# A hybrid decoder step on one core: shorter inverse roots, a one-instruction softmax bias, the MLP's first product in a written order, and new orders for all engines

## The chip, the cores and the metric

The kernel runs on one core of a Trainium2 chip. The metric is the device time of one execution in microseconds (us), median of several runs. Below, PE is TensorE's matmul queue, ACT is ScalarE, DVE is VectorE, POOL is GpSimd, and SP is the queue from which most DMAs are issued.

## The reference

One layer, for 256 prompt tokens and 8 sequences of 8 sample tokens, width 1024, all in float32:

```
h  = rmsnorm(x);  q, k, v, z, xbc, dt = h @ W_in
attention: MoBA, 8 heads of 64. A query scores the mean key of each past block of 256 tokens, keeps
           the best 3 and its own block, and takes softmax(q k) v over those. The prompt attends to
           itself, a sample sequence to 1024 past tokens (paged cache) and to itself. q, k: rmsnorm, rotary
ssd:       Mamba-2: causal convolution of width 4, silu, chunked scan over 8 heads of 64 (state 128)
           with a state carried in and out; y * silu(z), rmsnorm
x1 = x  + concat(attention, ssd) @ W_out
x2 = x1 + cross_attention(rmsnorm(x1), rmsnorm(mem)) @ W_o     (4 heads of 128, 256 memory tokens)
y  = x2 + relu(rmsnorm(x2) @ W_up)**2 @ W_down                 (width 4096)
```

It returns y for both groups, the new keys and values, the memory's keys and values, and the new convolution and ssd states.

## The kernel before

**Tiling.** Activations lie transposed, 128 features on the partitions by T = 320 tokens, eight tiles for the width of 1024. A weight chunk (`wr`, 128x1024, 512 KB) is loaded by a DMA on SP's or ACT's queue (`load`, L335), rounded to fp32r by ACT (`wh`, L387), and the rest is taken by DVE (`wl`, L388). `gemm3` forms hi*hi, hi*lo and lo*hi, so a product with one output tile is 24 matmuls (L393 to L395) of 128x320, given out as four units of six. Activations are split the same way by `split` (ACT L530, DVE L531). The values come first, in `V` units (L710 to L714). The first kernel rows also do the table load for ACT's exponential (L318) and warm-up matmuls (L538, fed by a POOL memset).

**Norms.** The scale of an rmsnorm isn't applied to the input but to the product: sums of squares are gathered on DVE (`acc`, L491), summed over partitions on PE (`means`, L498), and `rsqrt` takes the inverse root on DVE: an integer guess (L470), then three Newton rounds of three instructions (L472 to L474), on tiles of 3 to 24 columns. `spread` turns the columns into a row over all partitions with PE (L371). `qk_factors` does this for x (units F0 to F2) and for the heads of q (F3 to F5: `to_tokens` copies the sums on ACT at L509 and L511 and transposes them on PE, L371; then `rsqrt`, a copy at L611, and PE's `spread`) and of k (F6 to F9, the same with `dt_part`, L729 and on, between). `cross_factors` (X) does it for the cross attention's heads, `gated_norm` and `memory` have one root each, and `up_factor` the last, of x2.

**Order.** Each part of the work is a generator whose steps are units of PE work. `ORDER` is a string with one letter a unit; `weave_by` takes the next unit of the letter's generator, so PE's order is written out by hand. The letters that matter here: F `qk_factors`, Q the q and k products, V values, S `sample_attn`, T `prompt_attn`, B xbc products and their convolution, D and R the ssd, X `cross_factors`, G the product qx and then ox. Where a unit is numbered below (B28), it is counted from 0 in its generator. DVE's, ACT's and the DMAs' orders are written as runs of numbers (`DVE_ORDER`, `ACT_ORDER`, `DMA_ORDER`), which `_issue_order` makes into dependencies. POOL's order is free. All DMAs take turns on eight semaphores, so one waits for the landing of that eight places earlier, and a DMA on ACT's queue holds up what follows there.

**The MLP.** Up to the residual after ox everything comes from `ORDER`. The up product runs in `weave("", ...)`: a planner gives out the units of `up_factor` (F) and `G_up` (G) by estimated durations and lags. The first four products are held in PSUM (two buffers of `mm`, two of `as`) until the factor `rb3` is there, then `up_done` empties them: DVE relu and scale (`t`), ACT the square rounded (`hh`), POOL the square (L1683), DVE the rest (`hl`). From product 9 on each product also takes one step of `states_sample`, which updates the sample's ssd states. The down product follows.

**The sample attention's bias** is made in `sample_attn` by two DVE instructions, the maximum times -0.125 (L891) and that added to the block bias (L892).

Of the kernel before, what the change touches and what calls it, by code (L numbers as in the profile page):

```python
# [13 lines left out]
ALU = mybir.AluOpType  # L14
# [33 lines left out]
for _n, _c in (("g_mix", 8), ("g_x", 8), ("g_mem", 8), ("g_mlp", 8), ("g_ssm", 4),  # L48
# [40 lines left out]
DVE_ORDER = ("0+2 17 4 3 5 18 6+1 19 8 10+1 9 12+1 20 14+1 21 16 22+2 27 32 35 25+1 36 28 30 29 31 53 33+1 37 39 38 40+8 54 "  # L89
# [161 lines left out]
def _body(tc, nc, I, O):  # L251
# [215 lines left out]
    def rsqrt(out, x):  # L467

        t = ti(out.shape[-1])
        V.tensor_scalar(out.bitcast(I32), x.bitcast(I32), -0.5, MAGIC, op0=ALU.mult, op1=ALU.add)  # L470
        for _ in range(3):
            V.scalar_tensor_tensor(t, out, -0.5, out, op0=ALU.mult, op1=ALU.mult)  # L472
            V.tensor_tensor(t, t, x, op=ALU.mult)
            V.scalar_tensor_tensor(out, t, 1.5, out, op0=ALU.add, op1=ALU.mult)  # L474
# [1289 lines left out]
```

## Time and profile before

| | |
|---|---|
| median of 3 runs | 514.2 us (513.79 to 515.15) |
| the profiled execution's own time | 513.36 us |
| its span in the profile | 511.6 us |
| busy: PE, PE weight load | 499.2, 452.5 us |
| busy: DVE, ACT, POOL | 342.1, 252.4, 47.8 us |
| granted TensorE clock | 0.999 |
| read and written | 109.71 MB and 6.14 MB |

Busy times are sums over the records of each engine; PE's matmuls are pipelined, so a record is longer than the step from one start to the next. The profile lists waits by the releaser that came last, and a timeline row ends with the engine's idle time before it and what ended that. Stretches by window: the values and q, k products to 65 us, both attentions, convolution and ssd to 170, the mixer's output to 215, the memory and the cross attention to 280, and the MLP from there on.

### The profile page before, as it was taken

Reading aid. Unit: us, or ns where it says so; the run is one execution under the profiler, and the core shown is the slowest. Engines: PE = TensorE matmul, PEld = TensorE weight load, DVE = VectorE, ACT = ScalarE, POOL = GpSimd, SP = SyncE. Lnnn points to the kernel's source line nnn. Section 1 sums busy time; section 2 is a strip of 40 time slices with the busy share of each in tenths; the row PEclk is TensorE's granted clock in tenths of the full one; section 3 lists DMA queues with packets and bytes.
Section 4 is the critical chain, followed back from the end, with each engine's and each line's share of the span. In section 5 each row is a group of like instructions: output and inputs, shape, how many; then the busy total and the mean of one; then the engine's idle time right before and its main releaser. Section 6 shows DMA issues by size and latency. Waiting matters only on the chain.

```text
span 511.6 us, 10525 instructions
## 1 busy us (share of the span) xinstructions
PE 499.2 (98%) x3954; PEld 452.5 (88%) x3954; DVE 342.1 (67%) x697; ACT 252.4 (49%) x520; POOL 47.8 (9%) x90
## 2 busy tenths in 40 slices
PE   8999999999999999999999999999999999999997
PEld 5978777877767789999688999999999999999997
DVE  6868799685787799955749778766766433433431
ACT  8534436958667956635566344334344233232330
POOL 2500000030100000000000124222221000000000
PEclk9999999999999999999999999999999999999999
DMA  8999999899899155895904475554644455554530
GB/s 285 318 366 357 368 346 328 306 379 377 285 395 376 66 166 177 285 357 175 400 7 124 124 273 184 179 192 163 207 164 132 157 178 141 173 174 149 170 96 13
DMA packets 45364, 116.53 MB, mean 228 GB/s; under 512 B 5058, under 2 KB 7234, under 8 KB 45314
## 3 DMA queue, kind: packets, MB, share of 16 engines
q1 hardware_dynamic: 39266, 94.37, 54.1%
q10 hardware_dynamic: 6048, 21.50, 11.7%
q8 instruction: 31, 0.51, 0.4%
q14 instruction: 19, 0.16, 0.1%
HBM read 109.71 MB, written 6.14 MB: 226 GB/s over the span
## 4 chain that ended last, share of the span: by engine, by line
PE 84%; ACT 6%; DVE 5%; DMA 2%; issue 1%; SPq 0%; ACTq 0%; DVEq 0%
PE mm L393 22%; PE mm L394 21%; PE mm L395 21%; PE as L925 2%; PE sc L872 2%; DMA wr<-w 2%; PE ms L371 2%; PE as L371 1%; ACT wh L387 1%; DVE wl L388 1%; PE sc L710 1%; PE sc L1546 1%; PE sc L1548 1%; PE as L1570 1%; PE mm L1620 1%
## 5 line engine op out<-in xcount | busy, mean ns | idle before, releaser
L387 ACT ACTIVATE wh<-wr 128x1024 fp32r<-128x1024 f32 (+1 forms) x115 | 118.9, 1037 | 173.6 <-PE mm L394 103.8
L388 DVE TENSOR_TENSOR wl<-wr,wh 128x1024 fp32r<-128x1024 f32 (+1 forms) x115 | 144.1, 1256 | 83.0 <-ACT wh L387 81.0
L393 PE MATMUL mm<-big,wh 128*128 128x320 f32 x544 | 172.2, 316 | 0.8 <-DVE t L991 0.8
L395 PE MATMUL mm<-big,wl 128*128 128x320 f32 x544 | 168.1, 309 | 0.0
L394 PE MATMUL mm<-big,wh 128*128 128x320 f32 x544 | 168.1, 309 | 0.1
L393 PEld LDWEIGHTS mm<-big,wh 128*128 128x128 f32 x544 | 102.2, 188 | 9.7 <-issue 5.9
L394 PEld LDWEIGHTS mm<-big,wh 128*128 128x128 f32 x544 | 102.3, 188 | 0.8 <-DVE big L1608 0.3
L395 PEld LDWEIGHTS mm<-big,wl 128*128 128x128 f32 x544 | 102.1, 188 | 0.1
L395 PE MATMUL mm<-hh,wl 128*128 128x320 f32 x256 | 78.9, 308 | 0.0
L394 PE MATMUL mm<-hl,wh 128*128 128x320 f32 x256 | 78.9, 308 | 0.0
L393 PE MATMUL mm<-hh,wh 128*128 128x320 f32 x256 | 78.9, 308 | 0.0
L394 PEld LDWEIGHTS mm<-hl,wh 128*128 128x128 f32 x256 | 48.0, 188 | 0.0
L393 PEld LDWEIGHTS mm<-hh,wh 128*128 128x128 f32 x256 | 48.0, 188 | 0.0
L395 PEld LDWEIGHTS mm<-hh,wl 128*128 128x128 f32 x256 | 48.0, 188 | 0.0
L1683 POOL TENSOR_TENSOR t<-t 128x320 f32<-128x320 f32 x32 | 28.4, 887 | 160.9 <-DVE t L1680 152.0
L1680 DVE SCALAR_TENSOR_TENSOR t<-mm,rb 128x320 f32<-128x320 f32 x32 | 15.7, 489 | 15.1 <-PE mm L395 14.7
L1684 DVE TENSOR_TENSOR hl<-t,hh 128x320 fp32r<-128x320 f32 x32 | 15.4, 481 | 3.1 <-POOL t L1683 3.1
L872 PE MATMUL sc<-kv,qs 128*32 128x256 f32 x256 | 16.1, 382 | 0.4 <-DVE m L876 0.4
L1681 ACT ACTIVATE hh<-t 128x320 fp32r<-128x320 f32 x32 | 14.7, 458 | 3.7 <-DVE t L1680 3.7
L998 DVE SCALAR_TENSOR_TENSOR t<-t,cwh,t 128x320 f32<-128x320 f32 x24 | 13.2, 549 | 4.4 <-ACT t L996 2.3
L1346 DVE TENSOR_TENSOR x2T<-mm,x2T 128x320 f32<-128x320 f32 x8 | 3.9, 492 | 17.8 <-PE mm L395 17.8
L925 PE MATMUL as<-kv,p 128*32 128x256 f32 x256 | 15.3, 382 | 0.0
(356 smaller groups left out, 619.4 us busy)
## 6 DMA issues: line engine op xcount, KB each, us to landing
wr<-w SPq DMA_DIRECT2D x69, 512.0 KB, 3.5
wr<-w ACTq DMA_DIRECT2D x41, 512.0 KB, 4.8
kv<-ckT SPq DMA_DIRECT2D x64, 256.0 KB, 5.1
kv<-cv SPq DMA_DIRECT2D x64, 256.0 KB, 6.0
kv<-mk SPq DMA_DIRECT2D x8, 512.0 KB, 5.2
kv<-mv SPq DMA_DIRECT2D x8, 512.0 KB, 6.9
kv<-h SPq DMA_DIRECT2D x4, 512.0 KB, 8.0
big<-h SPq DMA_DIRECT2D x4, 512.0 KB, 5.1
```

The costliest lines, as they stand in the source:

```text
L371: PE.transpose(out, in_, ident[:n, :n])
L387: A.activation(hi[:, c], raw[:, c], AF.Copy)
L388: V.tensor_tensor(lo[:, c], raw[:, c], hi[:, c], op=ALU.subtract)
L393: PE.matmul(out, hi[:, cols], xh, start=start, stop=False)
L394: PE.matmul(out, hi[:, cols], xl, start=False, stop=False)
L395: PE.matmul(out, lo[:, cols], xh, start=False, stop=stop)
L872: PE.matmul(ps[r:r + 32, 256 * n:256 * n + 256], qs[:, s, g, b0 + e, :], kbs[e][:, :, 128 * (2 * g + s):128 * (2 * g + s) + 128], start=s ...
L925: PE.matmul(yv[r:r + 32, 0:256], pT[:, 2 * n + q, r:r + 32], vbs[e][:, q, 256 * g:256 * g + 256], start=n == 0 and q == 0, stop=first and ...
L1680: V.scalar_tensor_tensor(t, ps[:, :T], 0.0, rb3, op0=ALU.max, op1=ALU.mult)
L1681: A.activation(hh[:, m, :], t, AF.Square)
L1683: G.tensor_tensor(f, t, t, op=ALU.mult)
L1684: V.tensor_tensor(hl[:, m, :], f, hh[:, m, :], op=ALU.subtract)
```

## The change

1. `rsqrt` takes 8 instructions for 10: a first step with a quadratic correction (four instructions) and a second with a scaled Newton round (three).
2. The softmax bias is one instruction (L901 after), with the maximum broadcast; only the first of the four groups of sequences keeps the separate product.
3. The up product, the up factor and the states' steps are streams of `ORDER`: `!` opens the MLP's buffers, `u` gives the units of products 0, 2 and 4 to 31, `w` those of 1 and 3, `r` the factor, `t` the states. `up_done` is called at once where the factor is there, and otherwise by the second `r` unit.
4. POOL's order is written too (`POOL_ORDER`), and all other orders are new.

Lines after stand 6 to 10 below those before. In the core of the diff the tables of numbers are left out:

```diff
-ORDER = ("FVVVVQQQQQQQQQQQQQVQQFVQFVFQFQQQFVQQQQQSSQQQFSSQQQZQZSSFSFSVSSQFFBBBBSZBSBFBBSBBTZSBSSBBBSSBBTBTTBBS"
-         "SBSBSSBBSSSBTSSTBZSZBBSSBBTBTSZBBTSTBDSSSSZSDZSZDDZDSSZSDSDDSDTDDZZDDSDSZDDSZRSSSSSRSSRRMORORWRORWRO"
...
-         "cbabbaacMbcaddcddadcdGGKGGGGWGGGGGGGGGGG")
+ORDER = ("VFVVVQQQQQQQQQQQQQQVQFVQFQVFQFQQQFVQQQQSSQQQFSSQQQZQZSSFSFSVSSQFFBBBBSZBSZBBSFBBTBBSSSBBBSSBBTBTBBTS"
+         "SBSBBSSBSSSBSTSTBZSZBBSSBTBBZBBTSDBZSSDSSSTSZSZDDZTDSSZSDDSDDSDTDZZDDSDSZDDSZRSSSSSRRSRRSMOOROWRRWOR"
...
+         "babbXaaMbccdadcdddacdGGGGGGKGGGGGWGGGGGG!uuuwuruuuuwwrwwwwuwuuuuuuuuuuuuuuuuuuuutuuuuuuuutuuutuuuuuu"
+         "uuuuuuutuuutuuuuutuuutututuuuuuuutuuuuutuuuuuuuuuutuuuttuuutuuutuuutuuuuuuuuuuuuuuuuuuuu")
...
+POOL_ORDER = ("13 0+1 3 5 8 4 7 11 2 6 12 18 9+1 14 26 15+2 25 19+2 23+1 22 28 27 46 29 32 31 30 35+1 47 34 37 33 44 38+2 42 "
...
         V.tensor_scalar(out.bitcast(I32), x.bitcast(I32), -0.5, MAGIC, op0=ALU.mult, op1=ALU.add)
-        for _ in range(3):
-            V.scalar_tensor_tensor(t, out, -0.5, out, op0=ALU.mult, op1=ALU.mult)
-            V.tensor_tensor(t, t, x, op=ALU.mult)
-            V.scalar_tensor_tensor(out, t, 1.5, out, op0=ALU.add, op1=ALU.mult)
+        V.scalar_tensor_tensor(t, out, -0.5, out, op0=ALU.mult, op1=ALU.mult)
+        V.tensor_tensor(t, t, x, op=ALU.mult)
+        V.scalar_tensor_tensor(t, t, 5.0 / 3, t, op0=ALU.add, op1=ALU.mult)
+        V.scalar_tensor_tensor(out, t, 1.25, out, op0=ALU.add, op1=ALU.mult)
+        V.scalar_tensor_tensor(t, out, -1.6875, out, op0=ALU.mult, op1=ALU.mult)
+        V.tensor_tensor(t, t, x, op=ALU.mult)
+        V.scalar_tensor_tensor(out, t, 2.25, out, op0=ALU.add, op1=ALU.mult)
...
         V.reduce_max(t1, m5[:, 0:n5], axis=AX.X)
-        V.tensor_scalar(t1, t1, -0.125, None, op0=ALU.mult)
-        V.tensor_scalar(b5[:, 0:n5], b5[:, 0:n5], t1, None, op0=ALU.add)
+        V.scalar_tensor_tensor(b5[:, 0:n5], t1.broadcast_to((P, n5)), -0.125, b5[:, 0:n5], op0=ALU.mult, op1=ALU.add)
+        if first:
+            V.tensor_scalar(t1, t1, -0.125, None, op0=ALU.mult)
...
-    def states_sample(first):
-
-
+    def states_sample():
+
+        yield {"mlp"}, 0
...
                 V.tensor_tensor(by_head(h2), by_head(h2), el_s[:, 8 * c:8 * c + 8, None].broadcast_to((P, 8, 64)), op=ALU.mult)
-                yield
+                yield 0, 0
                 V.tensor_tensor(h2, h2, hps[q], op=ALU.add)
                 S.dma_start(O["ssm_s"][c], h2)
-                yield
+                yield 0, 0
 
...
-    weave(ORDER, F=qk_factors(), X=cross_factors(), S=att[0], N=norm(), D=ys[0], R=ys[1], T=att[1], a=crs[0], b=crs[1], c=crs[2], d=crs[3],
-          M=memory(), Q=G_mixer(), V=G_v(), B=G_xbc(), Z=G_z(), O=G_oa(), J=G_os(), G=G_all(), K=G_kx(), W=G_vx())
-    x3h, x3l = x4[0][:, 0], x4[0][:, 1]
-    xT = x2T[0]
-    xe_ = made["xe"]
-    rt3 = tl(xe_, [P, 3], "rt3")
-    rb3 = tl(xe_, [P, T], "rb3")
+    stD = ExitStack()
+    mlp = {}
+    def to_mlp():
+        p1s.close()
+        pm = pool("mlp", st=stD, side="right", reuse_waits="tile")
+        mlp["h"] = tl(pm, [P, 32, T], "hh", F32R), tl(pm, [P, 32, T], "hl", F32R)
+        mlp["rt"] = tl(made["xe"], [P, 3], "rt3")
+        mlp["rb"] = tl(made["xe"], [P, T], "rb3")
+        told.add("mlp")
+        yield 0, 0
     def up_done(m):
         def done(ps):
+            hh, hl = mlp["h"]
             t = tm(T)
-            V.scalar_tensor_tensor(t, ps[:, :T], 0.0, rb3, op0=ALU.max, op1=ALU.mult)
+            V.scalar_tensor_tensor(t, ps[:, :T], 0.0, mlp["rb"], op0=ALU.max, op1=ALU.mult)
             A.activation(hh[:, m, :], t, AF.Square)
             f = tm(T)
             G.tensor_tensor(f, t, t, op=ALU.mult)
             V.tensor_tensor(hl[:, m, :], f, hh[:, m, :], op=ALU.subtract)
         return done
-    p1s.close()
-    stD = ExitStack()
-    pm = pool("mlp", st=stD, side="right", reuse_waits="tile")
-    hh = tl(pm, [P, 32, T], "hh", F32R)
-    hl = tl(pm, [P, 32, T], "hl", F32R)
+    late = []
     def up_factor():
-        yield 0, 1.5
+        yield {"mlp"}, 0
         x = ti(3)
         means(x, rsq, T)
-        rsqrt(rt3, x)
+        rsqrt(mlp["rt"], x)
         yield 0.65, 3.0
-        ps = spread(lambda t: rt3[:, t:t + 1].broadcast_to((P, P)), range(3))
-        A.activation(rb3, ps[:, :T], AF.Copy)
+        ps = spread(lambda t: mlp["rt"][:, t:t + 1].broadcast_to((P, P)), range(3))
+        A.activation(mlp["rb"], ps[:, :T], AF.Copy)
         told.add("rb3")
+        for m, ps in late:
+            up_done(m)(ps)
         yield 0.45, 0
-    def G_up():
-        late = []
-        for m in range(32):
-            done = up_done(m)
-            if "rb3" not in told:
-                yield from gemm(CH["up"] + m, tiles(x3h), tiles(x3l), T, late.append, al=mm if m < 2 else sa_ps)
-                if "rb3" in told or m == 3:
-                    yield {"rb3"}, 0
-                    for i, ps in enumerate(late):
-                        up_done(i)(ps)
-                continue
-            yield from gemm(CH["up"] + m, tiles(x3h), tiles(x3l), T, done)
-            if m >= 9:
-                next(states, None)
-    states = states_sample(3)
-    weave("", F=up_factor(), G=G_up())
+    def G_up(ms_):
+        yield {"mlp"}, 0
+        for m in ms_:
+            def done(ps, m=m):
+                if "rb3" in told:
+                    up_done(m)(ps)
+                else:
+                    late.append((m, ps))
+            yield from gemm(CH["up"] + m, tiles(x4[0][:, 0]), tiles(x4[0][:, 1]), T, done, al=mm if m < 2 or m > 3 else sa_ps)
+    weave(ORDER, F=qk_factors(), X=cross_factors(), S=att[0], N=norm(), D=ys[0], R=ys[1], T=att[1], a=crs[0], b=crs[1], c=crs[2], d=crs[3],
+          M=memory(), Q=G_mixer(), V=G_v(), B=G_xbc(), Z=G_z(), O=G_oa(), J=G_os(), G=G_all(), K=G_kx(), W=G_vx(),
+          **{"!": to_mlp(), "r": up_factor(), "u": G_up([0, 2] + list(range(4, 32))), "w": G_up([1, 3]), "t": states_sample()})
+    xT = x2T[0]
+    hh, hl = mlp["h"]
...
+                       (lambda i: i.engine == mybir.EngineType.Pool, POOL_ORDER),
```

Three places. On ACT, the start of the program: `tab` is the tile on which the table is loaded early, `prm` the norms' weights, `big` the split input, L478 (L487 after) a sum of squares. Before:

```order
L340 DMA prm_81<-prm 128x8
L318 ACT_TABLE_LOAD
L318 ACTIVATE tab_78<-tab_78 128x1
L530 ACTIVATE big_116<-big_84,prm_81 128x320
L478 ACTIVATE acc_188<-big_84 128x320
L387 ACTIVATE wh_118<-wr_87 128x512
L530 ACTIVATE big_116<-big_84,prm_81 128x320
L478 ACTIVATE t_191<-big_84 128x320
L552 ACTIVATE kv_117<-big_116 128x2x64
```

After:

```order
L346 DMA prm_81<-prm 128x8
L539 ACT_TABLE_LOAD
L539 ACTIVATE big_116<-big_84,prm_81 128x320
L393 ACTIVATE wh_118<-wr_87 128x512
L539 ACTIVATE big_116<-big_84,prm_81 128x320
L487 ACTIVATE t_199<-big_84 128x320
L393 ACTIVATE wh_118<-wr_87 128x512
L561 ACTIVATE kv_117<-big_116 128x2x64
L487 ACTIVATE acc_196<-big_84 128x320
```

The first ACTIVATE was that on `tab`, which needs nothing but a memset; now it is the first split, which reads `prm`, and the table load comes with it. Sums of squares stand behind the second weight half.

On ACT around F3 and F4, `s` (L509, L511; L518, L520 after) being the copy of q's sums that the transposes of F4 read, and L335 (L341) a weight DMA. Before:

```order
L387 ACTIVATE wh_544<-wr_542 128x1024
L639 ACTIVATE rb_179<-ms_428 128x320
L478 ACTIVATE sq_420<-mm_348 128x320
L335 DMA wr_743<-w 128x1024
L509 ACTIVATE s_82_452<-ms_447 128x320
L511 ACTIVATE s_82_452<-ms_447 128x64
L335 DMA wr_768<-w 128x1024
L387 ACTIVATE wh_583<-wr_581 128x1024
```

After:

```order
L393 ACTIVATE wh_446<-wr_444 128x1024
L648 ACTIVATE rb_179<-ms_426 128x320
L341 DMA wr_739<-w 128x1024
L393 ACTIVATE wh_512<-wr_510 128x1024
L487 ACTIVATE sq_418<-mm_348 128x320
L518 ACTIVATE s_86_463<-ms_458 128x320
L520 ACTIVATE s_86_463<-ms_458 128x64
L341 DMA wr_764<-w 128x1024
L393 ACTIVATE wh_579<-wr_577 128x1024
```

The DMA just ahead of the copies has moved ahead of a weight copy and a square.

On DVE around T0, `tq` with `cst` (L780; L789 after) being the mask added to the prompt attention's scores, which empties their PSUM, L991 (L1001) and L998 (L1008) a convolution's evacuation and its taps. Before:

```order
L991 TENSOR_TENSOR t_1063<-mm_1029,rb_179 128x40x8
L388 TENSOR_TENSOR wl_1289<-wr_1286,wh_1288 128x1024
L956 SCALAR_TENSOR_TENSOR yn_937<-yn_937,ab_1011,ts_1082 128x256
L998 SCALAR_TENSOR_TENSOR t_1068<-t_1063,cwh_158,t_1068 128x320 x3
L780 TENSOR_TENSOR tq_1127<-ms_1104,cst_82 128x384
L780 TENSOR_TENSOR tq_1130<-ms_1105,cst_82 128x384
L780 TENSOR_TENSOR tq_1135<-as_1106,cst_82 128x384
L780 TENSOR_TENSOR tq_1138<-as_1107,cst_82 128x384
L1010 SCALAR_TENSOR_TENSOR t_1168<-mm_767,rb_179 128x320
```

After:

```order
L394 TENSOR_TENSOR wl_1283<-wr_1280,wh_1282 128x1024
L966 SCALAR_TENSOR_TENSOR yn_931<-yn_931,ab_1005,ts_1068 128x256
L1011 SCALAR_TENSOR_TENSOR big_84<-t_991,t_985 128x320
L1001 TENSOR_TENSOR t_1077<-mm_1023,rb_179 128x40x8
L394 TENSOR_TENSOR wl_1391<-wr_1388,wh_1390 128x1024
L789 TENSOR_TENSOR tq_1127<-ms_1104,cst_82 128x384
L789 TENSOR_TENSOR tq_1130<-ms_1105,cst_82 128x384
L789 TENSOR_TENSOR tq_1135<-as_1106,cst_82 128x384
L789 TENSOR_TENSOR tq_1138<-as_1107,cst_82 128x384
L790 TENSOR_REDUCE pmx_202_1124<-tq_1130 128x3
```

A second weight split has come in just ahead of the masks, and the convolution's taps and z's evacuation have moved away from there.

More of the change, by code (lines that the diff above doesn't have):

```diff
@@ L69 @@
 PACE = 1.3
-ORDER = ("FVVVVQQQQQQQQQQQQQVQQFVQFVFQFQQQFVQQQQQSSQQQFSSQQQZQZSSFSFSVSSQFFBBBBSZBSBFBBSBBTZSBSSBBBSSBBTBTTBBS"
-         "SBSBSSBBSSSBTSSTBZSZBBSSBBTBTSZBBTSTBDSSSSZSDZSZDDZDSSZSDSDDSDTDDZZDDSDSZDDSZRSSSSSRSSRRMORORWRORWRO"
-         "OWNOOWNONOOOOOMOONNOWONJJJJJJJJZJJJJJMWJJKOJKKKKKKKKKKGKKKKKWGMXGacJMGGGGGGGMGWGGGGGGMXXbcXXaabcadcb"
-         "cbabbaacMbcaddcddadcdGGKGGGGWGGGGGGGGGGG")
-ACT_ORDER = ("1 0 2 19 3+1 20 6 5 7 21 8+1 22 10+5 23 18 16+1 24+2 28 30 33 32 27 37 34 29 47 38 31 50 41 48 36 35 57 39+1 "
[14 rows of a table removed]
-DVE_ORDER = ("0+2 17 4 3 5 18 6+1 19 8 10+1 9 12+1 20 14+1 21 16 22+2 27 32 35 25+1 36 28 30 29 31 53 33+1 37 39 38 40+8 54 "
[18 rows of a table removed]
-DMA_ORDER = ("0+15 19+1 16+2 21+2 29+1 27 31+6 28 38+16 64 24 55+1 65 25 66 57+4 75 26 62 67+6 84 74 76+7 63 86+1 85 88+3 "
[4 rows of a table removed]
+ORDER = ("VFVVVQQQQQQQQQQQQQQVQFVQFQVFQFQQQFVQQQQSSQQQFSSQQQZQZSSFSFSVSSQFFBBBBSZBSZBBSFBBTBBSSSBBBSSBBTBTBBTS"
+         "SBSBBSSBSSSBSTSTBZSZBBSSBTBBZBBTSDBZSSDSSSTSZSZDDZTDSSZSDDSDDSDTDZZDDSDSZDDSZRSSSSSRRSRRSMOOROWRRWOR"
+         "OWNOOWNONOOOOOMOONNOOWNJJJJJJJJJJMJZJJWJJKJKKKKKKKKKKKKKKKWGGOGGMaXcGJMGGGGGMGWGGGGGGMXXbcXaabcadcbc"
+         "babbXaaMbccdadcdddacdGGGGGGKGGGGGWGGGGGG!uuuwuruuuuwwrwwwwuwuuuuuuuuuuuuuuuuuuuutuuuuuuuutuuutuuuuuu"
+         "uuuuuuutuuutuuuuutuuutututuuuuuuutuuuuutuuuuuuuuuutuuuttuuutuuutuuutuuuuuuuuuuuuuuuuuuuu")
+ACT_ORDER = ("1+3 20 5+1 19 21 7 0 8+2 22 11+3 16+1 23 15 24 28 30 33 18 27 25 32 26 29 38 34 43 37 31 50 39 36 57 44 35 "
[15 rows of a table added]
+DVE_ORDER = ("0+3 17 4+1 18 6+1 9 8 19 10 12 14+1 13 11 20+1 27 32 25 22 26 35 23 28 16 30 36 31 29 51 24 33 37 34 39+1 38 "
[19 rows of a table added]
+DMA_ORDER = ("1+2 0 4+11 19+1 16+2 21+1 29+4 23 34+1 24 36 28 37+5 45 43 46 44 47+6 64 54 25+1 55+3 65 59+2 27 66 62 75 67+4 "
[5 rows of a table added]
+POOL_ORDER = ("13 0+1 3 5 8 4 7 11 2 6 12 18 9+1 14 26 15+2 25 19+2 23+1 22 28 27 46 29 32 31 30 35+1 47 34 37 33 44 38+2 42 "
+              "45 43 49 41 48 50+1 53 52 54+31")
 TAKEN = []
@@ L1226, in states_sample @@
                 S.dma_start(hb[:, b:b + 2, :], I["h0"][b:b + 2].rearrange("b p c -> p b c"))
-        for _ in range(first):
-            yield
+        yield 0, 0
         for e in range(2):
@@ L1241, in states_sample @@
                 V.tensor_tensor(by_head(h2), by_head(h2), el_s[:, 8 * c:8 * c + 8, None].broadcast_to((P, 8, 64)), op=ALU.mult)
-                yield
+                yield 0, 0
                 V.tensor_tensor(h2, h2, hps[q], op=ALU.add)
                 S.dma_start(O["ssm_s"][c], h2)
-                yield
+                yield 0, 0
     def gated_norm():
@@ L1666, in _body @@
     ys = all_of("y", ssd_all(), ssd_rest())
-    weave(ORDER, F=qk_factors(), X=cross_factors(), S=att[0], N=norm(), D=ys[0], R=ys[1], T=att[1], a=crs[0], b=crs[1], c=crs[2], d=crs[3],
-          M=memory(), Q=G_mixer(), V=G_v(), B=G_xbc(), Z=G_z(), O=G_oa(), J=G_os(), G=G_all(), K=G_kx(), W=G_vx())
-    x3h, x3l = x4[0][:, 0], x4[0][:, 1]
-    xT = x2T[0]
-    xe_ = made["xe"]
-    rt3 = tl(xe_, [P, 3], "rt3")
-    rb3 = tl(xe_, [P, T], "rb3")
+    stD = ExitStack()
[7 more added lines that the diff above has]
+        told.add("mlp")
+        yield 0, 0
     def up_done(m):
         def done(ps):
+            hh, hl = mlp["h"]
             t = tm(T)
-            V.scalar_tensor_tensor(t, ps[:, :T], 0.0, rb3, op0=ALU.max, op1=ALU.mult)
+            V.scalar_tensor_tensor(t, ps[:, :T], 0.0, mlp["rb"], op0=ALU.max, op1=ALU.mult)
             A.activation(hh[:, m, :], t, AF.Square)
```

75 rows, old and new, of tables (ACT_ORDER, DMA_ORDER, DVE_ORDER) are left out of this document.

## The prediction

> **What bounds the kernel now.** I read the page's head first, for who is busy, then the stretches of the span, then the list of waits of TensorE, and then the timeline at each place where TensorE waits.
>
> ```profile
> span 511.6 us, 10525 instructions
> PE 499.2 (98%) x3954; PEld 452.5 (88%) x3954; DVE 342.1 (67%) x697; ACT 252.4 (49%) x520; POOL 47.8 (9%) x90
> ...
> PE 84%; ACT 6%; DVE 5%; DMA 2%; issue 1%; SPq 0%; ACTq 0%; DVEq 0%
> ```
>
> The first line is the span, the second each engine's busy time, the third the chain of work that ended last. TensorE is idle for 511.6 - 499.2 = 12.4 us, and that is all a new order can win, since the diff adds and removes no matmul. By stretch (TensorE's busy time stands after the length; the DMA share stands second from the right):
>
> ```profile
> 36.00:70.00 34.00, 31.35 (x296) 24.98 (x297) 27.16 (x88) 14.00 (x32) 1.08 (x5) 1.00 1.00 365
> ...
> 285.00:512.00 227.00, 223.21 (x1538) 221.84 (x1536) 122.86 (x149) 76.25 (x93) 28.40 (x32) 1.00 0.50 159
> ```
>
> From 285 us on, the MLP, TensorE misses 227.00 - 223.21 = 3.8 us, nearly all of it after its last matmul, where the diff touches nothing. The places to look at lie before. These are TensorE's waits by releaser (in total, times, longest; left out are the warm-up's own and one of 0.2 us that no term uses):
>
> ```profile
> PE ms L371 <- ACT s L509: 1.8, 2, 1.2
> PE ms L371 <- DVE ts L611: 1.4, 2, 0.8
> ...
> PE ms L498 <- DVE acc L491: 1.0, 1, 1.0
> PE mm L393 <- DVE t L991: 0.8, 1, 0.8
> PE as L371 <- DVE tq L780: 0.5, 1, 0.5
> PE sc L872 <- DVE m L876: 0.4, 1, 0.4
> PE as L713 <- ACT big L530: 0.4, 1, 0.4
> PE ms L1077 <- ACT rx L1056: 0.3, 1, 0.3
> ...
> PE as L371 <- ACT yn L960: 0.2, 1, 0.2
> PE ms L1077 <- ACT gm L1196: 0.2, 1, 0.2
> ```
>
> No row of TensorE names a DMA. A dozen single waits hold about 8 us, each for ScalarE or VectorE, engines busy for half and two thirds of the span. So the time is set by whether a small result is early enough, and order decides it. A wait costs about 0.16 more than its row, because a matmul's record outlasts its turn (0.31 against the 0.15 from one start to the next); I add 0.16 where I price one, and a unit of a product, six such matmuls, takes 0.88.
>
> ```profile
> 140.16 0.31 PE L393 MATMUL mm<-big,wh 128*128 128x320 f32 x1
> 140.31 0.31 PE L394 MATMUL mm<-big,wh 128*128 128x320 f32 x1
> ```
>
> **The change, part by part.** All sums are against the profiled execution, 513.36 us (span 511.6 and 1.76 around it). The median of the runs shown is 514.2, 0.8 above it.
>
> *Factors F3 to F5.* PE's L371 at 38.28 spreads a factor that ScalarE (L509) copies late, because that copy stands behind a weight DMA on ScalarE's own queue:
>
> ```profile
> 37.41 0.33 ACTq L335 DMA_DIRECT2D wr<-w  x1
> ...
> 37.79 0.44 ACT L509 ACTIVATE s<-ms 128x320 f32<-128x320 f32 x1 [3.05 <-DMA wr<-w]
> ...
> 38.28 0.55 PE L371 MATMUL ms<-cst,s 128*128 128x128 f32 x3 [1.23 <-ACT s L509]
> ...
> 41.41 0.18 DVE L474 SCALAR_TENSOR_TENSOR fr<-ti,fr 128x24 f32<-128x24 f32 x1
> ...
> 42.06 0.41 PE L371 MATMUL ms<-cst,ts 128*128 128x128 f32 x2 [0.61 <-DVE ts L611]
> ```
>
> After, the DMA is issued three rows earlier, a weight copy and a square stand between, and TensorE has one q unit between F3 and F4 (about 0.9 us of six matmuls). I take 1.15 of the 1.39 back; bounds 0 (the copy again behind a DMA) and 1.39. At F5 TensorE waits for the inverse root, whose links stand 0.22 apart on VectorE; two links fewer give 0.43 of the 0.77, taken as 0.4. Bounds 0 and 0.77.
>
> *F8 to F9.* The same root in `dt_part`'s company: its links share VectorE with a second chain.
>
> ```profile
> 65.40 0.18 DVE L470 TENSOR_SCALAR ti<-ti 128x24 int32<-128x24 int32 x1
> ...
> 67.88 0.69 DVE L611 COPY ts<-ti 128x256 f32<-128x256 f32 x3
> ...
> 68.31 0.86 PE L371 MATMUL ms<-cst,ts 128*128 128x128 f32 x5 [0.82 <-DVE ts L611]
> ```
>
> From L470 to the copies are 18 instructions in 2.48 us; the new row has 12 (two links gone, four of the other chain moved behind the copies). Dependent links need about 0.2 each, so 1.8 to 1.95: I take 0.6; bounds 0 and 0.98. The roots in the gated norm, memory and cross factors are no row of the waits; 0 to 0.4 for the cross factors, taken as 0.2, the others nothing, since products stand between them and their readers.
>
> *B27 to B28.* B28's product waits for a PSUM buffer, which VectorE empties (L991) only after S30's maxima:
>
> ```profile
> 121.62 0.48 DVE L991 TENSOR_TENSOR t<-mm,rb 128x320 f32<-128x320 f32 x1
> ...
> 122.15 0.41 PE L393 MATMUL mm<-big,wh 128*128 128x320 f32 x1 [0.82 <-DVE t L991]
> ```
>
> In the new ORDER T6 stands between B27 and B28, and VectorE has L991 earlier. I take 0.95 of 0.98, plus 0.2 just behind it. Bounds 0 and 1.2.
>
> *The ssd stretch, 140 to 170 us.* m L876, rx L1056, yn L960, gm L1196: 1.1 in rows, 1.7 with the additions. In the new ORDER a D or R unit is put between each producer and its reader. I take 1.3, since four places must all work; bounds 0 and 1.7.
>
> *Up factor.* The last residual's sum of squares is late by 1.18 because the planner puts the means two units after it:
>
> ```profile
> 280.35 0.48 DVE L491 TENSOR_TENSOR acc<-acc,sq 128x320 f32<-128x320 f32 x1
> ...
> 280.89 0.83 PE L498 MATMUL ms<-cst,acc 128*128 128x8 f32 x6 [1.02 <-DVE acc L491]
> ```
>
> Now `r` stands after `uuuwu`, five units of 0.88, three more than before: 2.6 us of cover for 1.18. I take 1.1. If that cover fails, 0. The second `r` comes six units later, more than the root and its spread need. The four products held back till then occupy two buffers each of two pools; they are emptied before the next one of those pools begins. The states' units (`t`) start later, but the whole stretch leaves VectorE 104 us of idle time by the windows above, so they cost nothing; without that cover they'd delay `hl` and the down product by their own work.
>
> *Start.* ScalarE's first work:
>
> ```profile
> 1.19 1.28 ACT L318 ACT_TABLE_LOAD   x1 [1.19 <-PEq L1756]
> 2.48 0.20 ACT L318 ACTIVATE tab<-tab 128x1 f32<-128x1 f32 x1
> ...
> 3.43 0.56 ACT L530 ACTIVATE big<-big,prm 128x320 fp32r<-128x320 f32 x1 [0.74 <-DMA prm<-prm]
> ...
> 5.46 1.36 PE L710 MATMUL sc<-wh,big 128*128 128x512 f32 x4
> ...
> 6.51 0.63 ACT L387 ACTIVATE wh<-wr 128x512 fp32r<-128x512 f32 x1 [0.46 <-DMA wr<-w]
> ...
> 7.92 0.50 PE L710 MATMUL sc<-wl,big 128*128 128x512 f32 x1 [0.23 <-DVE wl L388]
> ```
>
> The load now stands behind the wait for `prm` (over at 3.43), so the first split begins at 4.71 and the first weight half is copied at about 5.8: TensorE's first product begins 0.4 later, its next ones more. But the second half arrives by DMA at 6.5 as before, and TensorE waits at 7.92 for what hangs on that; most is absorbed there, and I keep 0.1. Splits and sums of squares change places on VectorE, 0.2 late for the third k tile and Q4. The wait for L530 (0.51 with the addition) goes, because the copy it hangs on stands ahead of a weight split. Sum: a gain of 0.2; bounds a gain of 0.5 and a loss of 1.3 (the load's whole length). The Trainium skill, "ScalarE: Activation LUTs", section "What ACT_TABLE_LOAD costs", puts beside a load of 1283 ns a drain of about 1380 ns, 2.66 us for a switch. This trace has the 1.28 and no drain: the next ACTIVATE begins 1.29 us after the load. By the page's number the start would lose some 1.3 us more, by the row nothing.
>
> *What the new orders put in the way.* T0's mask adds free the PSUM that S13 writes:
>
> ```profile
> 34.30 1.22 DVE L388 TENSOR_TENSOR wl<-wr,wh 128x1024 fp32r<-128x1024 f32 x1
> ...
> 82.95 1.01 DVE L780 TENSOR_TENSOR tq<-as,cst 128x384 f32<-128x384 f32 x2
> ...
> 83.55 0.44 PE L371 MATMUL as<-cst,yn 128*128 128x128 f32 x2 [0.49 <-DVE tq L780]
> ...
> 127.79 1.09 ACT L387 ACTIVATE wh<-wr 128x1024 fp32r<-128x1024 f32 x1
> ```
>
> The first line is from elsewhere, for the price of a weight split, and the last for that of a weight copy. Before, no split stood just ahead of the mask adds; in the new row one does (a split takes 1.22, first line), while two convolution steps move behind. I take 0.75 of loss; bounds 0 and 1.3. At S19 ScalarE has T0's last scaling, T1's second copy and S13's last copy between S17's exponentials (0.49 + 0.49 + 0.18 = 1.16): loss 0.65, bounds 0 and 1.2. At T8 a weight copy of 1.09 (last row) stands ahead of T5's last scaling: loss 0.7, bounds 0 and 1.1. At V6 0.15. *Softmax bias:* one instruction of some 0.2 less in each group after the first, in a chain beside products: nothing, unless the sample attention's exponentials are what TensorE waits for; there, 0.15 a time, inside the bounds. *GpSimd's order:* busy for 9%, one convolution's copy ahead of another's, about 1 us on chains with more than that to spare: nothing.
>
> Gains 1.15 + 0.4 + 0.6 + 0.2 + 0.95 + 0.2 + 1.3 + 1.1 + 0.2 = 6.1; losses 0.75 + 0.65 + 0.7 + 0.15 = 2.25. So 513.36 - 3.85 = 509.5 for a profiled execution, and with the median's 0.8, 510.3 us.
>
> **The rivals.**
> *The new waits don't come.* The three losses rest on where ScalarE and VectorE are by then; if the earlier gains leave them ahead, the 2.1 us drop out: 508.2. For it: both engines idle for 33% and more. Against: each place has its order row.
> *The waits only move.* TensorE, freed at F4, arrives earlier at the next unit whose inputs are set by landings and by VectorE, which in 36 to 70 us is busy for 27.16 of 34.00. If half the gains return as waits a few units on, 513.36 - 3.05 + 2.25 is 512.6, in median 513.4, no change that shows. This is also the case that the change does not do what it says.
> *Slower: a DMA on ScalarE's queue stops the engine.* Such a weight DMA waits for the landing of an earlier transfer, and everything behind it on ScalarE waits too; one place shows 3.05 us of it.
>
> ```profile
> wr<-w ACTq DMA_DIRECT2D x41, 512.0 KB, 4.8
> ```
>
> There are 41 of them, their places are all rewritten, and between 36 and 70 us the DMA share is 1.00. One new stop of 3 us with a reader 0.9 us behind costs 2.1; from two the gain is gone, with three the time is 510.3 + 6.3 = 516.6. Against it: no wait of TensorE but F4's hangs on one, and the new orders put more rows between.
> *The load with a drain.* What the page's number would do: 1.3 us more at the start, 511.6. The row at 2.48 speaks against it.
>
> **How the numbers follow.** Within 0.3% (1.5 us, about what a measurement of this kernel can tell from no change) is 512.7 to 515.7. Forecast, 509 to 512.5: 0.50. No new waits, 507 to 509: 0.20. Drain: 0.05. Waits moved: 0.14, same. Stopped ScalarE: 0.11, slower. Faster is 0.50 + 0.20 + 0.05 = 0.75. The range 507.2 to 514.2 leaves out the slower case, a third of the moved waits and a corner below, 0.2 in all; its low end is 513.36 - 7 + 0.8, all gains at their upper bounds and no losses.
>
> **What would show it.** In the profile after, the rows of s L509 (1.2 part), t L991 and acc L491 are gone from TensorE's waits, ts L611 is under 0.8, m, rx, yn and gm are gone or halved, and tq L780 has grown to about 1.0. The first L710 product begins near 5.9, with the table load at 3.4, and TensorE is idle for 8 to 9 us in all. I am wrong if TensorE gets new waits over 1 us for ScalarE with a DMA ahead of it, if the first product comes after 6.5, or if new waits between 80 and 135 us sum to more than 3.

## The result and the profile after

| | before | after |
|---|---|---|
| median | 514.0 us (513.23 to 515.15, 6 runs) | 509.64 us (508.55 to 510.69, 6 runs) |
| ratio, 95% interval | | 0.9915 (0.9897 to 0.9934) |
| profiled execution, its span | 513.36, 511.6 us | 510.33, 508.5 us |

The change makes the kernel 0.85% faster. The forecast was 510.3 us, in a range of 507.2 to 514.2. A second set on another chip gave 509.55 and a ratio of 0.9899 (0.9866 to 0.9931), experiment 12. The profiled execution lies at the slow end of its six; most of that is its start, see below.

The page and TensorE's waits after:

```profile
PE 499.4 (98%) x3954; PEld 454.5 (89%) x3954; DVE 335.8 (66%) x680; ACT 252.3 (50%) x520; POOL 56.8 (11%) x90
...
PE mm L399 <- DVE t L1692: 1.6, 3, 0.8
PE ms L377 <- ACT s L518: 0.6, 1, 0.6
PE ms L377 <- DVE ts L620: 0.4, 2, 0.2
PE as L935 <- ACT p L921: 0.4, 1, 0.4
PE ms L1126 <- ACT ti L1162: 0.3, 1, 0.3
PE ms L513 <- ACT sq L487: 0.2, 1, 0.2
```

Left out of the list, as in the prediction, is the warm-up's own wait, 1.9 us for 1.4. TensorE's busy time is the same, its idle time 9.1 us for 12.4. Of the long list of before, the copy s at F4, the residual's sum (acc), the PSUM of B28 (L991), the mask adds (tq), the split of L530, m, rx, yn and gm are gone; the two waits on the roots' copies (ts, at F5 and F9) are 0.4 together for 1.4. At the top stands a wait that before didn't have: L1692, the relu that empties the up product's PSUM, three times. By stretch:

```profile
36.00:70.00 34.00, 33.38 (x308) 26.30 (x308) 28.74 (x85) 14.65 (x34) 1.33 (x3) 1.00 0.99 350
...
285.00:508.50 223.50, 218.56 (x1501) 216.50 (x1499) 118.69 (x148) 74.42 (x92) 34.38 (x32) 1.00 0.48 159
```

From 36 to 70 us TensorE misses 0.6 us for 2.65; from 285 on 4.9 for 3.8. The table sets the forecast beside the traces. Its last column is worked out from the start times of the matmuls' records, at places where both programs have done the same matmuls: the change of the time between two such places, after minus before. Two of the places lie inside a wait: of the 1.20 from 42 to 63 us, 0.33 is what is left of F5's wait, and of the -1.62 from 263 to 284, 0.24 belongs to the end of the cross attention.

| stretch of before, us | terms of the prediction | forecast | measured |
|---|---|---|---|
| 0 to 14 | start | -0.2 | +0.29 |
| 14 to 42 | F4, F5, V6 | -1.4 | -2.00 |
| 42 to 63 | none | 0 | +1.20 |
| 63 to 68 | F9 | -0.6 | -0.59 |
| 68 to 83 | T0 | +0.75 | -0.73 |
| 83 to 122 | S19, B28 | -0.3 | -1.02 |
| 122 to 141 | T8, place behind B28 | +0.5 | -0.54 |
| 141 to 175 | ssd | -1.3 | +0.11 |
| 175 to 263 | cross factors | -0.2 | -0.55 |
| 263 to 284 | up factor | -1.1 | -1.62 |
| 284 to the end | none | 0 | +2.39 |
| sum | | -3.85 | -3.06 |

The sum came out well by luck, because two misses cancel: 2.1 us of losses at T0, S19 and T8 that did not come, against 2.4 us in the MLP that had no term. From 42 us on a second trace of the changed kernel (experiment 12) gives the same column within 0.1 us; ahead of that it is 0.95 us earlier, -2.66 for -1.71, so that its sum is -3.9.

### The profile page after: what moved, and what is told of

Read it like the earlier page. It is cut to its first block, busy times and chain, and to the rows that moved or that the text cites. A ratio compares the mean times of both kernels' runs of the same rounds, so it can differ in the third digit from the quotient of the medians.

```text
span 508.5 us, 10447 instructions
## 1 busy us (share of the span) xinstructions
PE 499.4 (98%) x3954; PEld 454.5 (89%) x3954; DVE 335.8 (66%) x680; ACT 252.3 (50%) x520; POOL 56.8 (11%) x90
## 4 chain that ended last, share of the span: by engine, by line
PE 82%; DMA 7%; DVE 6%; ACT 2%; issue 1%; SPq 1%; ACTq 0%; POOL 0%; DVEq 0%
PE mm L399 21%; PE mm L400 20%; PE mm L401 20%; DMA wr<-w 3%; DMA kv<-ckT 3%; PE sc L881 3%; PE as L935 2%; PE ms L377 2%; DVE wl L394 2%; PE as L377 1%; PE sc L1555 1%; DMA kv<-cv 1%; PE ms L1657 1%; PE as L1579 1%; PE sc L1556 1%
## 5 line engine op out<-in xcount | busy, mean ns | idle before, releaser
L394 DVE TENSOR_TENSOR wl<-wr,wh 128x1024 fp32r<-128x1024 f32 (+1 forms) x115 | 140.4, 1228 | 64.8 <-ACT wh L393 63.1
L399 PE MATMUL mm<-big,wh 128*128 128x320 f32 x528 | 167.2, 317 | 1.6 <-DVE t L1692 1.6
L400 PE MATMUL mm<-big,wh 128*128 128x320 f32 x528 | 163.2, 309 | 0.1
L401 PE MATMUL mm<-big,wl 128*128 128x320 f32 x528 | 163.2, 309 | 0.0
L399 PEld LDWEIGHTS mm<-big,wh 128*128 128x128 f32 x528 | 99.1, 188 | 10.5 <-issue 8.3
L400 PEld LDWEIGHTS mm<-big,wh 128*128 128x128 f32 x528 | 99.2, 188 | 1.1 <-DVE big L1289 0.6
L401 PEld LDWEIGHTS mm<-big,wl 128*128 128x128 f32 x528 | 99.1, 188 | 0.1
L400 PE MATMUL mm<-hl,wh 128*128 128x320 f32 x256 | 78.9, 308 | 0.0
L1695 POOL TENSOR_TENSOR t<-t 128x320 f32<-128x320 f32 x32 | 34.4, 1077 | 158.2 <-DVE t L1692 140.1
L400 PEld LDWEIGHTS mm<-hl,wh 128*128 128x128 f32 x256 | 48.0, 188 | 0.0
L1692 DVE SCALAR_TENSOR_TENSOR t<-mm,rb 128x320 f32<-128x320 f32 x30 | 14.5, 484 | 18.9 <-PE mm L401 15.5
L1696 DVE TENSOR_TENSOR hl<-t,hh 128x320 fp32r<-128x320 f32 x32 | 18.2, 596 | 12.8 <-ACT hh L1693 9.9
L1008 DVE SCALAR_TENSOR_TENSOR t<-t,cwh,t 128x320 f32<-128x320 f32 x24 | 13.2, 550 | 3.2 <-ACT t L1005 1.8
```

Of the source, the lines that this page charges most:

```text
L394: V.tensor_tensor(lo[:, c], raw[:, c], hi[:, c], op=ALU.subtract)
L399: PE.matmul(out, hi[:, cols], xh, start=start, stop=False)
L400: PE.matmul(out, hi[:, cols], xl, start=False, stop=False)
L401: PE.matmul(out, lo[:, cols], xh, start=False, stop=stop)
L1692: V.scalar_tensor_tensor(t, ps[:, :T], 0.0, mlp["rb"], op0=ALU.max, op1=ALU.mult)
L1695: G.tensor_tensor(f, t, t, op=ALU.mult)
```

## The experiments

Theory 1: a few small results came late, and the orders bring them earlier. Theory 2: VectorE has 17 instructions less, and that is the gain. The times of before beside the runs are 514.59 us (experiments 1 to 4), 515.22 (5 to 8) and 514.82 (9 to 12). Where one trace is compared with another, the ends of waits are meant, and not the times of single executions, which differ by more than a microsecond.

**1. The MLP's evacuations first** (VectorE's and ScalarE's orders between 284 and 330 us; one piece of each, products numbered by their output tile):

```diff
 DVE L1692 t (product 3)
+DVE L394 wl (product 5)
+DVE L1692 t (product 4)
 DVE L394 wl (product 6)
-DVE L1696 hl (product 1)
-DVE L394 wl (product 7)
-DVE L1692 t (product 4)
...
 ACT L393 wh (product 4)
-ACT L393 wh (product 5)
 ACT L1693 hh (products 0, 1, 2)
+ACT L393 wh (product 5)
```

> The changed kernel with 49 VectorE and 25 ScalarE places of the MLP rewritten: each up product's evacuation (the relu into t) stands ahead of weight splits and of the states' steps, and each rounded square (hh) ahead of the weight copy that waits for TensorE. Nothing else differs. Theory 1 (order: a late small result costs TensorE, whatever the engines' load): the three waits of TensorE on t in the MLP (0.96, 0.43 and 0.69 from start to start, 2.1 us in all) go, and the time falls by 1.5 to 2.1 us, to about 507.8. Rival (VectorE and GpSimd get in each other's way there, and the delay is theirs): t comes late all the same, weight splits become late instead, and the time falls by less than 0.7.

By the numbers in the orders, 22 of VectorE's places and 15 of ScalarE's differ, not 49 and 25.

Measured: 507.48 us (507.06 to 508.28, 6 runs), 0.9865 of before (0.9842 to 0.9887). No wait on L1692 is left; where the changed kernel's window from 285 to 330 us has 43.41 us of busy TensorE in 45.00, this one's waits for nothing:

```profile
285.00:326.00 41.00, 41.00 (x289) 40.45 (x288) 34.02 (x48) 17.34 (x25) 16.82 (x13) 1.00 0.57 188
```

Theory 1 holds here, and this is a kernel faster than both. The rows that it mends, in the changed kernel:

```profile
292.73 0.48 DVE L1692 SCALAR_TENSOR_TENSOR t<-as,rb 128x320 f32<-128x320 f32 x1
...
293.13 1.21 DVE L394 TENSOR_TENSOR wl<-wr,wh 128x1024 fp32r<-128x1024 f32 x1
293.29 1.63 POOL L1695 TENSOR_TENSOR t<-t 128x320 f32<-128x320 f32 x1 [0.83 <-DVE t L1692]
...
294.26 1.00 DVE L1696 TENSOR_TENSOR hl<-t,hh 128x320 fp32r<-128x320 f32 x1
...
295.19 1.21 DVE L394 TENSOR_TENSOR wl<-wr,wh 128x1024 fp32r<-128x1024 f32 x1
...
296.33 0.48 DVE L1692 SCALAR_TENSOR_TENSOR t<-mm,rb 128x320 f32<-128x320 f32 x1
...
296.95 0.39 PE L399 MATMUL mm<-big,wh 128*128 128x320 f32 x1 [0.80 <-DVE t L1692]
```

The evacuation at 296.33, for which TensorE waits, stands in VectorE's queue behind two weight splits and a remainder; products 6 and 7, for which the splits are, are begun only after it.

**2. The start's order of before.**

```diff
-ACT split of x tile 0 (brings the table load) ... ACT tab
+ACT tab (brings the table load), ACT split of x tile 0
-POOL memset v, tab, ts
+POOL memset tab, ts, v
```

> The changed kernel with the start's order of before in two places: the activation that brings the table load stands ahead of the first split, and GpSimd fills the warm-up's data ahead of the values' buffer. Theory 1: the load is over by 2.5 us again, the first product begins at 5.3 to 5.5 for 6.0, and the first q product at about 13.9 to 14.1 for 14.3: 0.2 to 0.4 us gained at the start, in all 0 to 0.4. If TensorE's slow first products (0.43 apart for 0.23) come from the later warm-up, they are 0.23 apart again from the second one on. Rival: the second weight half's landing at 6.5 sets the start whatever the order, and nothing changes behind 8 us.

Measured: 510.45 us (509.01 to 511.01, 4 runs), 0.9914 (0.9882 to 0.9946): no gain that shows. The load is early again and the first product begins at 5.59, but the second weight half landed only at 7.3 us in this execution, and the first q product begins at 14.63 (14.68 in the changed kernel's first trace). A gain of 0 to 0.4 us is less than four runs can tell, so what the table load's place is worth stays open; this trace goes with the rival, that the landing sets the start. From the second one on the first products are 0.23 apart; experiment 12 shows that this comes with the changed order too.

**3. The old root in the new orders.**

```diff
-rsqrt: 8 instructions
+rsqrt: 10 instructions, the last two behind the eighth's place
```

> The changed kernel with the inverse root of before (10 instructions for 8, in the same places, the two more right behind the last). Theory 1: 0.4 us more at F5, about 0.4 at F9 and up to 0.3 at the cross factors, 0.6 to 1.1 us in all: about 510.5. Theory 2 (the 17 fewer VectorE instructions make the gain): most of the 4.4 us of the change is lost again, and the time is 512.5 or more.

Measured: 510.23 us (510.08 to 510.85, 4 runs), 0.9921 (0.9892 to 0.9951). Of TensorE's waits only the one on the roots' copies grew, from 0.4 to

```profile
PE ms L377 <- DVE ts L617: 1.3, 2, 0.7
```

so two links at F5 and two at F9 are worth 0.9 us of wait together, and theory 2's 512.5 is excluded.

**4. The new arithmetic in the old orders.**

```diff
-rsqrt: 10 instructions; bias: 2
+rsqrt: 8 instructions; bias: 1 (after the first group), all in the places of before
```

> The kernel before, in its own orders, with the 8-instruction root and the one-instruction bias alone. Theory 1: 0.4 us at F5, up to 0.4 at F9, little elsewhere: 0.4 to 1.0 us less than before. Theory 2: most of the change's gain is here already, 3 us or more.

Measured: 513.87 us (512.03 to 516.18, 10 runs), 0.9991 (0.9969 to 1.0013): 0.5 us less than before by the ratio and 0.7 by the medians, with an interval that takes in no change. The trace has two waits that fell:

```profile
PE ms L371 <- ACT s L512: 1.2, 2, 0.7
...
PE ms L371 <- DVE ts L614: 1.0, 2, 0.8
```

ts from 1.4 to 1.0, F5's share, while F9's 0.8 stays: there the copies wait for the second chain, and only the new order takes that out of the way. s at F4 fell from 1.2 to 0.7 with no change of order there: the DMA ahead of it was issued at 37.07 us for 37.41, so a part of that wait differs between executions. By the ratio the arithmetic in the old orders is worth about a tenth of the change, by the interval a third at most; the rest needs the new orders.

**5. The means early again.**

```diff
-!uuuwuruuuu
+!uuruwuuuuu
```

> The changed kernel with the first r unit (the means of the up factor) after two units of the up product, as before, and not after five; all other orders are kept. Theory 1: the means wait for the last residual's sum of squares again, 1.0 to 1.2 us on TensorE, and behind it the root's link to the second r unit has three units more, so nothing else moves: the time rises by 1.0 to 1.4 us, to about 510.8. Rival (the wait was never on the path, the first evacuations set the MLP's start): less than 0.4.

Measured: 512.1 us (510.58 to 512.89, 10 runs), 0.9935 (0.9912 to 0.9958). The wait is back:

```profile
PE ms L507 <- DVE acc L500: 1.6, 1, 1.6
```

It is 1.6 and not 1.0 as before; TensorE, less held up ahead of it, comes sooner to the same sum. Against the changed kernel's trace about 1.7 us are lost there and 0.2 behind it, and 0.6 come back in the MLP, where L1692 has two waits for three; that third wait is also missing in experiments 6 and 8, and the last section says with what it comes. By the ratios, 0.9935 against 0.9915 and 0.9899, the loss is 1.0 to 1.9 us. The term stands: from before to the changed kernel the means come 1.19 us earlier there, for the 1.1 forecast.

**6. The weight DMA back at s.**

```diff
-ACT DMA wr_739
 ACT L393 wh_512
 ACT L487 sq_418
+ACT DMA wr_739
 ACT L518 s_86_463
```

> The changed kernel with the weight DMA that was moved ahead of a weight copy and a square put back just ahead of the copies s (L518), where it stood before. If its place makes the wait at F4, 1.0 to 1.4 us of wait on s come back at 38 us. If the landing that it waits for makes it (that of the transfer eight places earlier, 37.3 before, and by this trace over at 35.1 in the changed kernel's new order of DMAs), the copy is at most 0.2 late and TensorE waits 0.2 or less.

Measured: 509.22 us, one run, and no wait at F4:

```profile
33.98 0.33 ACTq L341 DMA_DIRECT2D wr<-w  x1
...
36.63 0.44 ACT L518 ACTIVATE s<-ms 128x320 f32<-128x320 f32 x1 [1.86 <-PE ms L513]
37.47 0.49 PE L377 MATMUL ms<-cst,s 128*128 128x128 f32 x3
```

The DMA, the last row ahead of s in ScalarE's order, issues 2.6 us before s (the square ahead of it begins only at 34.34), and s starts as soon as TensorE's sums are there. So its place alone isn't what made the wait of before. What is left is the landing that it waits for: before, the DMA could issue only at 37.41, in the changed kernel at 34.78 and here at 33.98. That is read from the traces, and no run undid the DMAs' order alone.

**7. GpSimd's order free.**

```diff
-POOL_ORDER = ("13 0+1 3 5 8 ...")
+POOL_ORDER = ""
```

> The changed kernel without a written order for GpSimd. GpSimd is busy for 11% and only fills buffers, copies convolution edges and squares in the MLP, in the same sequence there: theory 1 expects no change but at the start, where the warm-up's data come 0.6 us earlier: 0 to 0.3 us less. Rival (the written order keeps GpSimd out of VectorE's way): 0.5 us or more slower, with longer VectorE splits in the first 130 us.

Measured: 509.13 us (508.59 to 509.39, 4 runs), 0.9872 (0.9815 to 0.9928). The interval takes in the changed kernel's 0.9915: no loss, and a gain isn't shown.

**8. T0 one unit later.**

```diff
-ORDER: B7 B8 T0 B9 B10 S13
+ORDER: B7 B8 B9 T0 B10 S13
```

> The changed kernel with T0, the prompt attention's scores, one unit later in TensorE's order, so that one unit and not two stand between T0 and S13; VectorE's order, with a weight split ahead of the mask adds, is kept. If the unit between is what kept the predicted wait away, TensorE waits 0.6 to 1.0 us at S13 for the mask adds. If VectorE has room there, no wait over 0.2.

Measured: 510.13 us, one run, with the wait of before at S13:

```profile
80.83 1.02 DVE L789 TENSOR_TENSOR tq<-ms,cst 128x384 f32<-128x384 f32 x2 [1.01 <-PE as L781]
81.77 1.01 DVE L789 TENSOR_TENSOR tq<-as,cst 128x384 f32<-128x384 f32 x2
...
82.37 0.44 PE L377 MATMUL as<-cst,yn 128*128 128x128 f32 x2 [0.49 <-DVE tq L789]
```

VectorE itself waits 1.01 us for T0's scores, so the weight split ahead of the masks, on which the prediction's loss rested, is not in the way. The unit between T0 and S13 is what keeps the wait off.

**9. The first experiment with GpSimd's order free.**

```diff
 DVE_ORDER, ACT_ORDER: as in experiment 1
-POOL_ORDER = ("13 0+1 3 5 8 ...")
+POOL_ORDER = ""
```

> The changed kernel with the MLP places of the first experiment and without a written order for GpSimd. If both effects stand by themselves: 2.1 us less than the changed kernel from the MLP, and from the start whatever the free order gives (0 to 0.5): 507.0 to 507.6, the fastest of all here. If the written order keeps GpSimd out of VectorE's way, 508 or more.

Measured: 507.01 us (506.72 to 507.63, 6 runs), 0.985 (0.9819 to 0.988): the fastest, 2.5 us under the changed kernel on the same chip (experiment 12). Against experiment 1 (507.48, another chip) the intervals overlap, so the free order's own part stays open.

**10. ScalarE's part of the first alone.**

```diff
-ACT L393 wh (product 5)
 ACT L1693 hh (products 0, 1, 2)
+ACT L393 wh (product 5)
...
 DVE_ORDER: as in the changed kernel
```

> Of the first experiment only ScalarE's part: the rounded squares (hh) ahead of the weight copies in the MLP, VectorE's order as in the changed kernel. If the second wait on t (0.43 at 304) comes from squares held up by a weight copy that waits for TensorE, it goes, and the first (0.96 at 296) and the third (0.69 at 327), which come from VectorE's own order, stay: 0.4 us less. If all three come from the squares, all go.

Measured: 507.85 us, one run. Of TensorE's waits on t one is left, the third:

```profile
PE mm L399 <- DVE t L1692: 0.3, 1, 0.3
```

So the first wait, too, goes when the squares come in time: VectorE is then through its remainders sooner and reaches the relu at 294.10. To put it down to VectorE's order alone was wrong. That wait (0.80) stands in all eight traces that have the changed kernel's MLP orders, and the second in seven of them (not in experiment 7), so that ScalarE's order removed the second is likely and not shown by one run.

**11. VectorE's part alone, in two places.**

```diff
 DVE L394 wl (product 6)
+DVE L1692 t (product 4)
 DVE L1696 hl (product 1)
 DVE L394 wl (product 7)
-DVE L1692 t (product 4)
...
+DVE L1692 t (product 12)
 DVE L394 wl, L1696 hl, L1250 state
-DVE L1692 t (product 12)
```

> Of the first experiment only VectorE's part, and of that two places: one evacuation ahead of a remainder and a weight split (296 us), another ahead of a state's step (327 us). The first wait (0.96) and the third (0.69) go, the second (0.43 at 304) stays: 1.6 us less. If they stay, VectorE's order there wasn't the cause.

At the second place a remainder (L1696) also moves up, and a step of the states (L1252) down.

Measured: 508.44 us, one run. The same row is left, but the wait is the second, at 303: the first and third went. Either engine's order removes the first wait. The second stayed without ScalarE's part, and the third went with VectorE's; but the third is missing in experiments 5, 6 and 8 as well, without any change of the MLP's orders, so one run doesn't show whose it is (last section).

**12. The changed kernel again.**

> The changed kernel as it is, on the chip of the three others, for a second trace and a comparison on one chip. Its time should be 509.0 to 510.2. Its start tells whether the slow rate of the first products (0.43 from start to start in the first trace, 0.23 or 0.28 in others with the same rows) belongs to the program or to the execution: if to the execution, the first q product is anywhere from 13.6 to 14.4; if to the program, it is at 14.3 again.

Measured: 509.55 us (508.6 to 510.94, 6 runs), 0.9899 (0.9866 to 0.9931). The waits are those of the first trace, row by row, but not the start. First the changed kernel, then this second trace of it:

```profile
6.17 2.29 PE L719 MATMUL sc<-wh,big 128*128 128x512 f32 x4
8.29 0.63 PE L719 MATMUL sc<-wl,big 128*128 128x512 f32 x2
```

```profile
5.86 1.19 PE L719 MATMUL sc<-wh,big 128*128 128x512 f32 x4
6.89 0.61 PE L719 MATMUL sc<-wl,big 128*128 128x512 f32 x2
```

The same four products take 2.12 us to the next in one execution and 1.03 in the other, and the first q product starts 0.73 us apart, by the records' start times. So about 0.7 us of the first trace's start belong to the execution and not to the program.

## Why the prediction was right, and where its steps were wrong

**Start** (-0.2, measured +0.29): in the second trace the first q product comes 0.45 us ahead of before's instead (13.95 against 14.40). The load with a drain, the 2.66 us that the Trainium skill, "ScalarE: Activation LUTs", section "What ACT_TABLE_LOAD costs", gives, did not show: the load begins at 3.30, the split follows at 4.60.

```profile
3.30 1.28 ACT L539 ACT_TABLE_LOAD   x1 [3.30 <-DMA prm<-prm]
...
4.60 0.56 ACT L539 ACTIVATE big<-big,prm 128x320 fp32r<-128x320 f32 x1
```

**F4 and F5** (-1.4, measured -2.0): the place was right and the mechanism half. The wait hung on the weight DMA, but not on the rows between it and s (experiment 6), and the whole wait came back. L371 at 38.28 is the transposes of q's sums, and not the spread of a factor that the prediction calls it. Of F5's 0.77 the root's two links took the share forecast; 0.33 of it is left, in the next row.

**42 to 63 us** (0, measured +1.20): the rival of waits that move. Besides F5's 0.33, 0.76 lies in S0: TensorE comes to it earlier, and its products take longer, by the chain below because of the cache's transfers. Before, and after:

```profile
48.64 1.93 PE L872 MATMUL sc<-kv,qs 128*32 128x256 f32 x32
```

```profile
47.26 2.70 PE L881 MATMUL sc<-kv,qs 128*32 128x256 f32 x32
```

The chain of work after runs through transfers there: 

```profile
37.52 6.60 DMA wr<-w
44.14 3.80 DMA kv<-cv
47.94 2.02 PE sc L881 x30
```

A part of what F4 gave is bounded by landings. That transfers bind there is read from the chain and was not tried by itself.

**F9** (-0.6, measured -0.59): right, and by the mechanism told; experiments 3 and 4 show that it needs the fewer links and the moved copies together.

**T0, S19, T8** (+2.1 together): wrong, and the one failed step is the same three times: I compared what stands ahead of the writer on VectorE and ScalarE with the reader's place of before. The readers had moved too: two units for one between T0 and S13, T3 behind B18, T8 behind S36. This is what the first rival, that the new waits don't come, gave as an outcome, with a chance of 0.20 and another reason. Experiment 8 shows it for T0; for the others only the trace speaks, with 0.4 on L921 left at 127 us.

**B28** (-0.95): right; no wait on L1001 is left.

**Ssd** (-1.3, measured +0.11): the four waits went, but new ones came in the same stretch, by the trace 0.3 for L1162 and, at O1, products that wait for their splits:

```profile
166.42 0.49 DVE L1289 TENSOR_TENSOR big<-big,big 128x320 fp32r<-128x320 f32 x1 [0.32 <-ACT big L1288]
166.44 0.42 PE L399 MATMUL mm<-big,wh 128*128 128x320 f32 x1
...
166.97 0.41 PE L400 MATMUL mm<-big,wh 128*128 128x320 f32 x1
```

L400 needs the remainder that L1289 writes, and follows after 0.53 for 0.15; some 0.9 us are lost there. The step "all four must work" asked whether the waits go, and not what is late next. No experiment was made on it.

**MLP** (0, measured +2.39): wrong. "The stretch leaves VectorE 104 us of idle time" was true and said nothing: an idle engine with a written order still does the next instruction only when the one ahead of it can go. The squares waited behind a weight copy that waited for TensorE, the remainders for the squares, and the relu stood behind remainders and splits (experiments 1, 10 and 11). The three waits on the relu are 2.1 of the 2.39, from start to start.

**Softmax bias and GpSimd's order** at nothing: no experiment shows otherwise, though experiment 7's interval leaves room for a gain of up to 1%.

**The range.** Its low end was said to be all gains at their upper bounds, 7 us. The bounds as given add up to about 8.1 (1.39 + 0.77 + 0.98 + 0.4 + 1.2 + 1.7 + 1.18 + 0.5), which would make it 506.0 and not 507.2. The result lies inside either way.

## What to carry to other kernels

Where one engine is busy for 98%, list its single waits, and for each ask what stands ahead of the late instruction in its own queue and how many units lie between writer and reader after the change; both ends move when orders are rewritten. A rewritten order also binds engines that are half idle: put the instruction that frees the bottleneck's buffer ahead of work for later units. That was worth 2.1 us here, half as much as the whole change.

## What was not expected of the hardware

The rate of the first products differs between executions of one program: 0.43 us from start to start for two of them in the first trace, 0.23 in the second, while the profile's clock says 1.00 in both. The Trainium skill, "TensorE: Matmul & The Clock Gate", part 1, has a gate that opens only after a busy window of about 3.4 us, and windows that run freely; that fits a switch at 5 to 8 us here that doesn't follow the program, but the gate itself isn't in these traces.

GpSimd and VectorE hold each other up in the MLP: GpSimd's square takes 0.72 us alone and 1.63 beside a weight split (293.29), VectorE's remainder 1.00 (294.26) for 0.48. The Trainium skill, "SBUF — State Buffer", section "Who interferes with whom", on the port pair that VectorE's instructions with two SBUF inputs and GpSimd's share, says that one blocks the other wholly; these rows agree as far as they go. That GpSimd is slower costs nothing in itself: in experiment 1 its squares take 1.16 us in the mean for 1.08, and that kernel is the faster one.

```profile
L1695 POOL TENSOR_TENSOR t<-t 128x320 f32<-128x320 f32 x32 | 37.0, 1159 | 153.3 <-DVE t L1692 146.4 <-ACT hh L1693 3.6 <-ACT wh L393 3.2
```

But a delay of VectorE can reach TensorE. Two weight splits stand together in VectorE's order at about 310 us, and a square of GpSimd comes due beside them. In the changed kernel, and then in experiment 6, which has the same MLP orders:

```profile
310.15 2.87 DVE L394 TENSOR_TENSOR wl<-wr,wh 128x1024 fp32r<-128x1024 f32 x2
310.40 1.54 POOL L1695 TENSOR_TENSOR t<-t 128x320 f32<-128x320 f32 x1 [3.53 <-DVE t L1692]
...
327.64 0.39 PE L399 MATMUL mm<-big,wh 128*128 128x320 f32 x1 [0.53 <-DVE t L1692]
```

```profile
309.58 2.35 DVE L394 TENSOR_TENSOR wl<-wr,wh 128x1024 fp32r<-128x1024 f32 x2
309.82 4.56 POOL L1695 TENSOR_TENSOR t<-t 128x320 f32<-128x320 f32 x2 [3.53 <-DVE t L1692]
```

In the first the square is through early and the second split takes 1.74 us for 1.21; in the other the square is held back, and the splits are not slowed. Both cases come with the same MLP orders. In the four traces with the slow split (the changed kernel twice, experiments 2 and 7) TensorE's third wait on L1692 is 0.52 to 0.53; in the four without it, it is 0.01 at most (experiments 5, 6 and 8) or 0.28 (experiment 3). In experiment 10, with VectorE's order of the changed kernel, the split is not slow and the wait is 0.29. In experiments 1, 9 and 11 the split is slow too and that wait does not come; there the relu stands ahead of later work. So about 0.5 us of the MLP's loss goes with which of the two engines comes first, unless the order leaves room for it. This is read from the traces; no run changed it alone.
